# A two-block transformer step on one core: softmax order in the attention, half buffers and late splits for the weights, and the skip term of the S5 mixer folded into its taps

## The chip, the cores and the metric

The kernel runs on one core of a Trainium2 chip. The metric is the device time of one launch in microseconds (us), median over the runs shown. The profile is of one execution of the program with the hardware profiler on.

## The reference, cut to what matters

Two blocks follow each other on a sequence of 256 positions with 1024 channels, all in float32. Each has two layers.

```
first:  h = h + short_conv_mixer(rmsnorm(h));  h = h + mlp(rmsnorm(h));  h = h + ple(rmsnorm(h), p[0])
        h = h + dilated_attention(rmsnorm(h)); h = h + mlp(rmsnorm(h));  h = h + ple(rmsnorm(h), p[1])
second: h = h + 0.5 swiglu(rmsnorm(h)); h = h + s5_mixer(rmsnorm(h));  h = h + 0.5 swiglu(rmsnorm(h))
        shared keys and values = rmsnorm(h) @ w_kv, some compressed
        h = h + 0.5 swiglu(rmsnorm(h)); h = h + nsa_attention(rmsnorm(h), kv);  h = h + 0.5 swiglu(rmsnorm(h))

dilated_attention, per head: three groups with dilations 1, 4, 16 share one softmax
  s = q k^T / sqrt(128), masked to a band;  p = exp(s - lse);  o = sum over groups of weight * (p v)
S5 mixer: x_t = A x_(t-1) + B u_t  (64 groups of 16 channels, 64 states)
  y = Re(C x) + d_skip * u;   y = gelu(y);   y * sigmoid(y @ w_glu)
swiglu: (silu(x @ w_a) * (x @ w_b)) @ w_out
rmsnorm(x) = x * rsqrt(mean(x^2) + eps) * gain
```

## The kernel before, in words

**Products.** Activations lie transposed, channels on the partitions, 256 positions on the free axis. A float32 product is made of three matmuls in a reduced format: each operand is split into a high part (`hi`) and a low rest (`lo`), and `mm3` (L328 on) issues hi·hi, lo·hi and hi·lo into one PSUM sum. They are lines L333, L334 and L335 of the profile.

**Weights.** All weight matrices stand in HBM as one row of pieces of 128 x 2048 elements (1 MB). `load` fetches them (tile `raw`), `split` makes `whi` on ScalarE (L267) and `wlo` on VectorE (L271), two halves of 1024 columns each; the four pieces after the S5 mixer's own are subtracted on GpSimd instead (L269, set `BY_POOL`). Each of `raw`, `whi`, `wlo` has a ring of three buffers. `piece` hands out the next split piece to a matmul block and, before it does so, splits up to three pieces ahead.

**Norms.** The factor of a norm isn't waited for: the matmuls run on the unscaled input, and a PSUM result is multiplied by the factor R afterwards. `norm_step` counts pairs of k tiles inside the matmul loops; at the first count the sums of squares are taken (`norm_ssq`), at the fifth a matmul spreads the factor over the partitions (L509, tile `misc`), ScalarE copies it out (L511, tile `R`). Evacuations that need R are put on the list `late` until then (`when_scaled`).

**Order.** A scheduler of the framework sorts the recorded instructions by a simulated timeline. Where the code says `in_order()`, an instruction is held behind the one recorded last on its engine. Each engine then works in that order and waits on semaphores.

**Attention** (L700 to L850). For each of eight heads: q, k, v pieces for three groups; rotary on q and k (VectorE L733 and L735, GpSimd L736, L738, L739, then `qh`, `ql`); v (`vh`, `vl`, L413, L414). `head` is a generator: scores, then the masked softmax (VectorE L771 to L779, ScalarE L781 exp, GpSimd L782 reciprocal, ScalarE L784 scaling), then the transposes of the probabilities on TensorE (L789 to L791), then the products with v. The `yield`s between them let the loop over pieces put matmuls of the next head in between.

**S5 mixer** (L1140 to L1330). The input h (tile `XG`, L1148, scaled by the gain) is transposed on TensorE (L1171), multiplied by the norm factor and goes through four quarter chains: `w` (input taps), `c` (rotation by GpSimd L1222 and L1226, VectorE L1220, L1221, L1227, scan L1223, result `sX` L1230), `t` and `o` (taps and output). `skip` multiplies XG by R on GpSimd (L1254, eight times), after ScalarE has multiplied it by d (L1279). `result` transposes the output back, adds XG (L1268), applies Gelu (L1272) and splits it (tiles `yh`, `yl`). The order of these steps is the string `S5_SEQ`. Then the GLU's matmuls follow, then the next SwiGLU, whose first input `xh`, `xl` is line L460.

Of the kernel before, what the change touches and what calls it, by code (L numbers as in the profile page):

```python
# [10 lines left out]
F32 = mybir.dt.float32  # L11
# [6 lines left out]
D = 1024  # L18
S = 256
# [29 lines left out]
SC_HEAD = SC_D + KT  # L49
# [6 lines left out]
S5_SEQ = "r0 r1 w0 r2 w1 r3 c0 w2 t0 c1 o0 w3 t1 t2 T o1 c2 t3 K o2 c3 R0 o3 R1 S"  # L56
# [143 lines left out]

BY_POOL = {S5_AT + S5_N + i for i in range(4)}
# [9 lines left out]
IN_ORDER = {E.DVE, E.Activation, E.Pool, E.PE}  # L211


class Ker:
    def __init__(self, ctx, tc, a):
# [13 lines left out]
        self.by_pool = BY_POOL  # L229
# [3 lines left out]
    def load(self, i):  # L233
        nc = self.nc
        while self.n_load < min(i, len(PLAN)):
            n, e = self.n_load, PLAN[self.n_load]
            if e[0] == "s5":

                m = (n - S5_AT) % 3
                t = self.ring.tile([128, NP_], F32R if m else F32, name=("raw", "whi", "wlo")[m])  # L240
                t = t.bitcast(F32) if m else t
                nc.sync.dma_start(t, self.s5w[e[1:]])
# [14 lines left out]
    def split(self, i):  # L257
        nc = self.nc
        while self.n_split < min(i, len(PLAN)):
            n = self.n_split  # L260
            assert PLAN[n][0] != "s5"
            self.load(n + 1)
            r = self.raw.pop(n)
            hi = self.ring.tile([128, NP_], F32R, name="whi")
            lo = self.ring.tile([128, NP_], F32R, name="wlo")
            for c in (slice(i, i + 1024) for i in range(0, NP_, 1024)):
                nc.scalar.activation(hi[:, c], r[:, c], AF.Copy)  # L267
                if n in self.by_pool:
                    nc.gpsimd.tensor_tensor(lo[:, c], r[:, c], hi[:, c].bitcast(F32), op=OP.subtract)  # L269
                else:  # L270
                    nc.vector.tensor_sub(lo[:, c], r[:, c], hi[:, c].bitcast(F32))  # L271
            self.spl[n] = (hi, lo)
            self.n_split += 1

    def piece(self, *want, ahead=3):
# [20 lines left out]
    def step(self):  # L296
# [3 lines left out]
        while self.credit >= 1.0:  # L300
# [36 lines left out]
    def cols_open(self, *want, ahead=3, ps="acc"):  # L337
        wh, wl = (w.rearrange("p (k c) -> p k c", k=KT) for w in self.piece("cols", *want, ahead=ahead))
        return self.psum(ps).rearrange("p (o t) -> p o t", o=2), wh, wl

    def cols_part(self, x, a, ks):
        acc, wh, wl = a
        for k in ks:
            for o in range(2):
                s = slice(128 * o, 128 * o + 128)
                self.mm3(acc[:, o], wh[:, k, s], wl[:, k, s], x[0][k], x[1][k],
# [9 lines left out]
    def cols_t(self, x, *want, ps="acc"):  # L356
        wh, wl = (w.rearrange("p (k c) -> p k c", k=KT) for w in self.piece("cols", *want))
        acc = self.psum(ps).rearrange("p (o t) -> p o t", o=2)
        for k in range(KT):
            for o in range(2):  # L360
                s = slice(128 * o, 128 * o + 128)
                self.mm3(acc[:, o], x[0][k][:, s], x[1][k][:, s], wh[:, k], wl[:, k],
# [30 lines left out]
    def rows(self, hid, dn, first, last, outs, *want):  # L393
        wh, wl = (w.rearrange("p (k c) -> p k c", k=2) for w in self.piece("rows", *want))
        for o in outs:
            for k in range(2):
                s = slice(128 * o, 128 * o + 128)
                self.mm3(dn[o // 2][:, o % 2], wh[:, k, s], wl[:, k, s], hid[0][:, k], hid[1][:, k],
                         first and k == 0 and o % 2 == 0, last and k == 1)
# [146 lines left out]
    def first_feed(self):  # L546
# [3 lines left out]
        hi, lo = (self.ring.tile([128, NP_], F32R, name=f"w{c}") for c in ("hi", "lo"))  # L550
        for j in range(4):
# [3 lines left out]
            self.hilo(r[:, c], hi[:, c], lo[:, c])  # L555
# [94 lines left out]
    def ple_proj(self, l, p):  # L650
# [3 lines left out]
        wh, wl = (w.rearrange("p (k c) -> p k c", k=2) for w in self.piece("rows", "ple_w_proj", l, 0))  # L654
        for j in range(4):
            acc = self.psum().rearrange("p (o t) -> p o t", o=2) if j > 1 else accs[j]
            for o in range(2):
                for k in range(2):
                    s = slice(256 * j + 128 * o, 256 * j + 128 * o + 128)
                    self.mm3(acc[:, o], wh[:, k, s], wl[:, k, s], p[0][:, k], p[1][:, k],  # L660
# [52 lines left out]
    def attention_(self, x):  # L713
# [40 lines left out]
        def head(h):  # L754
# [279 lines left out]
    def s5_weights(self, qs):  # L1034
# [5 lines left out]
        for q in qs:  # L1040
# [18 lines left out]
            for hf in range(2):  # L1059
# [46 lines left out]
                taps(1)  # L1106
                yield
# [29 lines left out]
    def s5(self, upd):  # L1137
# [3 lines left out]
        XG = big("XG", [2, 8, 4, 32])  # L1141
# [58 lines left out]
        wp = lambda n, q: self.piece("s5", n, q).rearrange("p (g c) -> p g c", c=128)  # L1200
# [37 lines left out]
        def wo(q):  # L1238
# [5 lines left out]
            for i in range(2):  # L1244
                evac(0, YP[0][:, :, 4 * q + 2 * i:4 * q + 2 * i + 2].rearrange("p j g h -> p g j h"),
# [617 lines left out]
```

## Time and profile before

| | |
|---|---|
| median of 3 runs | 1875.27 us (1873.52 to 1877.62) |
| profiled execution, its own time | 1871.9 us |
| its span | 1870.1 us |
| TensorE busy | 1817.1 us, 97% |
| VectorE / ScalarE / GpSimd busy | 69% / 50% / 25% |
| mean granted TensorE clock | 0.989 of 2.4 GHz |

TensorE works almost all the time. Time is lost in short waits of TensorE (a few us each) and in the short stretches at half the clock that come behind some of them. In 40 slices of the span, the busy share of TensorE is 9 tenths or more but for the first slice and two slices around 1050 to 1100 us, where the S5 mixer lies.

### The profile page before, as it was taken

The numbers are of one execution on the slowest core, as the hardware profiler recorded it, in microseconds if no ns is written. First come the engines' busy times: TensorE is split into PE (matmuls) and PEld (weight loads), VectorE is DVE, ScalarE is ACT, GpSimd is POOL, SyncE is SP. The second block draws the span as 40 slices with busy tenths as digits, with TensorE's granted clock in tenths as the row PEclk, the third lists the DMA queues.
The fourth block names the chain that finished last, engine by engine and source line by source line (L and its number), as shares of the span: only waits on it lengthen the run. The fifth ranks groups of instructions, "written<-read, shape, count | busy, mean of one in ns | idle before, by whom it ended". The sixth has DMA issues, their size and how long they took to land.

```text
span 1870.1 us, 35822 instructions
## 1 busy us (share of the span) xinstructions
PE 1817.1 (97%) x15244; PEld 1792.0 (96%) x15244; DVE 1281.1 (69%) x1633; ACT 942.3 (50%) x1442; POOL 468.5 (25%) x392
## 2 busy tenths in 40 slices
PE   8999999999999999999999779999999999999999
PEld 8999999999999999999999779999999999899999
DVE  6889887888776867778555566555785556875554
ACT  4365556555444555466443455444565445764442
POOL 2120012564652311112010442101243113421110
PEclk9999999999999999999999979999999999999999
DMA  6455666443343576666555734755455453445452
GB/s 253 181 187 209 220 223 219 161 152 142 136 144 127 198 236 227 219 207 254 188 186 187 291 128 172 263 185 186 174 187 200 173 183 118 65 161 181 181 180 90
DMA packets 78927, 344.68 MB, mean 184 GB/s; under 512 B 8022, under 2 KB 34378, under 8 KB 41392
## 3 DMA queue, kind: packets, MB, share of 16 engines
q1 hardware_dynamic: 77616, 339.30, 52.4%
q0 software_dynamic: 1008, 2.91, 0.4%
q8 instruction: 119, 1.95, 0.4%
q14 instruction: 40, 0.33, 0.1%
q10 hardware_dynamic: 144, 0.20, 0.0%
HBM read 328.71 MB, written 17.86 MB: 185 GB/s over the span
## 4 chain that ended last, share of the span: by engine, by line
PE 81%; DVE 7%; POOL 4%; issue 3%; ACT 2%; DMA 1%; SPq 0%; POOLq 0%; ACTq 0%; DVEq 0%
PE acc L334 16%; PE acc L335 16%; PE acc L333 16%; PE big L333 9%; PE big L334 9%; PE big L335 9%; DVE wlo L271 3%; POOL qks L736 2%; POOL qkt L739 1%; PE acc L1690 1%; POOL qkc L738 1%; ACT whi L267 1%; DMA bias<-zb 1%; PE big L1673 1%; PE misc L485 0%
## 5 line engine op out<-in xcount | busy, mean ns | idle before, releaser
L267 ACT ACTIVATE whi<-raw 128x1024 fp32r<-128x1024 f32 x558 | 559.8, 1051 | 599.8 <-issue 360.9
L271 DVE TENSOR_TENSOR wlo<-raw,whi 128x1024 fp32r<-128x1024 f32 x550 | 698.7, 1305 | 224.5 <-ACT whi L267 223.9
L334 PE MATMUL acc<-xl,whi 128*128 128x256 f32 x2096 | 595.7, 285 | 3.6 <-DVE xl L460 3.0
L333 PE MATMUL acc<-xh,whi 128*128 128x256 f32 x2096 | 594.5, 285 | 4.5 <-ACT whi L410 2.3
L335 PE MATMUL acc<-xh,wlo 128*128 128x256 f32 x2096 | 595.8, 285 | 3.0 <-DVE wlo L411 2.8
L333 PEld LDWEIGHTS acc<-xh,whi 128*128 128x128 f32 x2096 | 403.2, 193 | 6.4 <-ACT whi L410 2.7
L335 PEld LDWEIGHTS acc<-xh,wlo 128*128 128x128 f32 x2096 | 403.8, 193 | 5.3 <-DVE wlo L411 3.4
L334 PEld LDWEIGHTS acc<-xl,whi 128*128 128x128 f32 x2096 | 403.8, 193 | 4.8 <-DVE xl L460 3.4
L334 PE MATMUL big<-hl,whi 128*128 128x256 f32 x1216 | 343.6, 283 | 0.0
L335 PE MATMUL big<-hh,wlo 128*128 128x256 f32 x1216 | 343.2, 283 | 0.0
L333 PE MATMUL big<-hh,whi 128*128 128x256 f32 x1216 | 341.1, 284 | 0.0
L334 PEld LDWEIGHTS big<-hl,whi 128*128 128x128 f32 x1216 | 232.8, 191 | 0.5 <-issue 0.5
L335 PEld LDWEIGHTS big<-hh,wlo 128*128 128x128 f32 x1216 | 232.7, 191 | 0.2 <-issue 0.2
L333 PEld LDWEIGHTS big<-hh,whi 128*128 128x128 f32 x1216 | 231.0, 191 | 1.9 <-issue 1.9
L855 POOL TENSOR_TENSOR e<-e,R 128x512 f32<-128x512 f32 x44 | 80.6, 1833 | 524.5 <-ACT e L854 524.5
L335 PE MATMUL acc<-yh,wlo 128*128 128x256 f32 x720 | 204.1, 285 | 1.2 <-DVE wlo L271 1.0
L334 PE MATMUL acc<-yl,whi 128*128 128x256 f32 x720 | 204.1, 286 | 1.0 <-DVE yl L460 0.6
L333 PE MATMUL acc<-yh,whi 128*128 128x256 f32 x720 | 203.0, 286 | 0.8 <-ACT yh L410 0.5
L334 PEld LDWEIGHTS acc<-yl,whi 128*128 128x128 f32 x720 | 138.7, 193 | 2.0 <-DVE yl L460 1.3
L335 PEld LDWEIGHTS acc<-yh,wlo 128*128 128x128 f32 x720 | 138.9, 193 | 1.7 <-DVE wlo L271 1.2
L333 PEld LDWEIGHTS acc<-yh,whi 128*128 128x128 f32 x720 | 138.1, 194 | 2.2 <-ACT yh L410 1.3
L516 DVE TENSOR_TENSOR e<-acc,R 128x512 f32<-128x512 f32 x54 | 36.9, 689 | 84.4 <-PE acc L335 84.1
(440 smaller groups left out, 2592.4 us busy)
## 6 DMA issues: line engine op xcount, KB each, us to landing
raw<-in_wst SPq DMA_DIRECT2D x277, 1024.0 KB, 4.9
s5wo<-b SPq DMA_DIRECT2D x8, 512.0 KB, 5.7
s5wi<-wi SPq DMA_DIRECT2D x16, 256.0 KB, 3.7
s5to<-s5k SPq DMA_DIRECT2D x32, 128.0 KB, 4.5
bias<-zb SPq DMA_DIRECT2D x16, 256.0 KB, 4.5
cbt<-zb SPq DMA_DIRECT2D x4, 900.0 KB, 6.5
raw<-s5to SPq DMA_DIRECT2D x3, 1024.0 KB, 4.8
raw<-in_wst SPq DMA_DIRECT2D x4, 512.0 KB, 7.9
```

The source lines that it names most:

```text
L267: nc.scalar.activation(hi[:, c], r[:, c], AF.Copy)
L271: nc.vector.tensor_sub(lo[:, c], r[:, c], hi[:, c].bitcast(F32))
L333: mm(out, lh, rh, start=first, stop=False, skip_group_check=True)
L334: mm(out, lh, rl, start=False, stop=False, skip_group_check=True)
L335: mm(out, ll, rh, start=False, stop=last, skip_group_check=True)
L516: self.nc.vector.tensor_tensor(t, acc, self.bc2(self.R), op=OP.mult)
L736: nc.gpsimd.tensor_tensor(s, s, bc(self.rS), op=OP.mult)
L738: nc.gpsimd.tensor_tensor(c, t[:32], bc(self.rC), op=OP.mult)
L739: nc.gpsimd.tensor_tensor(t[:32], c, s, op=OP.add)
L855: nc.gpsimd.tensor_tensor(T[i], T[i], self.bc2(self.R), op=OP.mult)
L1673: nc.tensor.transpose(tp[:, 128 * n:128 * n + 128], blocks[4 * i + n], self.ident)
L1690: nc.tensor.matmul(o[:, dst], w, t[lp][:, e, b, src], start=False, stop=(b == 1 and kb == 1 and i == 2), skip_group_check=True)
```

## The change

Five things change.

1. In `head` the scores and the products with v are placed `in_order()`, the pause between scores and softmax is gone (another stands behind the softmax), and the nine transposes of a head are one ordered block with three PSUM tiles.
2. `whi` and `wlo` of a piece become two tiles of half the columns each (class `Halves`, ring of six).
3. Splits have places. `piece` puts the fetch of the next pieces (load and split) behind the evacuations on `late` while a norm factor is being made, in order; background steps pause as well. GpSimd makes no `wlo` any more.
4. `rows` walks over k first for all but the last block, so that the first half buffer is used up first.
5. In S5 the term d·u is added to the taps (`dd`, small products on GpSimd in the background work of an earlier stage), and `skip`, XG·d and the addition of XG go. Gelu moves into the evacuation of the output (L1163 before). XG lies in an outer pool. The three first GLU pieces are split at two named places (P and Q in `S5_SEQ`).

The core of the diff:

```diff
-S5_SEQ = "r0 r1 w0 r2 w1 r3 c0 w2 t0 c1 o0 w3 t1 t2 T o1 c2 t3 K o2 c3 R0 o3 R1 S"
+S5_SEQ = "r0 r1 w0 r2 w1 r3 T c0 w2 t0 c1 o0 w3 t1 t2 o1 c2 t3 o2 c3 P R0 o3 R1 Q S"
-BY_POOL = {S5_AT + S5_N + i for i in range(4)}
+class Halves:
+    def __init__(self, pool, name):
+        self.t = [pool.tile([128, NP_ // 2], F32R, name=name, bufs=6) for _ in range(2)]
...
-        self.split(min(i + ahead, self.cap))
-        self.load(i + ahead + 3 if d >= 0 or i + ahead < S5_AT else min(S5_AT + 3 * (i + ahead - S5_AT) + 3, S5_AT + 9))
+        def fetch():
+            self.split(min(i + ahead, self.cap))
+            self.load(i + ahead + 3 if d >= 0 or i + ahead < S5_AT
+                      else min(S5_AT + 3 * (i + ahead - S5_AT) + 3, S5_AT + 9))
+
+        if 0 < len(self.todo) < 4 and self.n_split >= i + 2:
+
+            self.late.append(lambda: self.behind(fetch))
+        else:
+            fetch()
...
-        while self.credit >= 1.0:
+        while self.credit >= 1.0 and not self.todo:
...
+    def behind(self, fn):
+        with self.in_order():
+            fn()
...
-        for o in outs:
-            for k in range(2):
-                s = slice(128 * o, 128 * o + 128)
+        for k, o in ([(k, o) for o in outs for k in range(2)] if last else [(k, o) for k in range(2) for o in outs]):
+            s = slice(128 * o, 128 * o + 128)
...
-                    self.mm3(dst[g], qh[:, 0, q0:q0 + 128], ql[:, 0, q0:q0 + 128],
-                             qh[:, 1, :nk], ql[:, 1, :nk], first, True)
-            yield
+                    with self.in_order():
+                        self.mm3(dst[g], qh[:, 0, q0:q0 + 128], ql[:, 0, q0:q0 + 128],
+                                 qh[:, 1, :nk], ql[:, 1, :nk], first, True)
...
             yield
+            yield
             PT = []
-            for g in range(3):
-                tp = self.psum("big")
-                nc.tensor.transpose(tp[:, 0:128], p0[:, g], self.ident)
...
+            with self.in_order():
+                tps = [self.psum("big") for _ in range(3)]
+                for g, tp in enumerate(tps):
+                    nc.tensor.transpose(tp[:, 0:128], p0[:, g], self.ident)
...
+                dd = bp.tile([16, 8, 16], F32, name="dd", bufs=1)
+                gp.tensor_tensor(dd, self.ident[:16, None, :16].to_broadcast([16, 8, 16]),
+                                 self.small[:16, SC_D + g0:SC_D + g0 + 8, None].to_broadcast([16, 8, 16]), op=OP.mult)
+                gp.tensor_tensor(ksb[:, :, :16], ksb[:, :, :16], dd, op=OP.add)
...
-        def skip():
-            self.norm_bc()
-            Ri = self.R.rearrange("p (c i) -> p i c", i=8)
-            for k in range(KT):
-                t = XG[:, k // 4, :, k % 4]
-                gp.tensor_tensor(t, t, Ri, op=OP.mult)
+        def presplit(c):
+            with self.in_order():
+                if c == 0:
+                    split.extend(self.split_open(3))
+                self.split_half(split, c)
...
-                v.tensor_tensor(dst[:, 4 * jb:4 * jb + 4], tp.rearrange("p (j g c) -> p j g c", j=4, c=32),
-                                XG[:, hf, 4 * jb:4 * jb + 4], op=OP.add)
-            for g in range(0, 4, 2):
-                k = 4 * hf + g
-                ac.activation(Y[0][:, k:k + 2], Y[0][:, k:k + 2], AF.Gelu_apprx_tanh)
+                evac(1 - jb, dst[:, 4 * jb:4 * jb + 4], tp.rearrange("p (j g c) -> p j g c", j=4, c=32))
```

ScalarE at the norm of the SwiGLU behind S5, before: R stands between splits, and the following piece was split ahead of it (`misc` is the spread factor, `e2` the Silu, `R` the factor, `whi` and `raw` weight pieces).

```order
L847 ACTIVATE e2_13026<-acc_12968 128x512
L267 ACTIVATE whi_13101<-raw_12859 128x1024 x2
L267 ACTIVATE whi_13163<-raw_12966 128x1024 x2
L511 ACTIVATE R_13053<-misc_13051 128x256
L854 ACTIVATE e2_13057<-e0_13055 128x512
L854 ACTIVATE e2_13160<-e0_13158 128x512
L267 ACTIVATE whi_13225<-raw_13034 128x1024 x2
L410 ACTIVATE hh_13097<-e2_13057 128x512
```

The same place in the changed kernel.

```order
L433 ACT_TABLE_LOAD
L433 ACTIVATE tab_13314<-ones_76 128x1
L879 ACTIVATE e2_13384<-acc_13326 128x512
L539 ACTIVATE R_13403<-misc_13401 128x256
L886 ACTIVATE e2_13407<-e0_13405 128x512
L289 ACTIVATE whi_13410<-raw_13213 128x1024
L289 ACTIVATE whi_13411<-raw_13213 128x1024
L289 ACTIVATE whi_13461<-raw_13215 128x1024
L289 ACTIVATE whi_13462<-raw_13215 128x1024
L289 ACTIVATE whi_13525<-raw_13324 128x1024
L289 ACTIVATE whi_13526<-raw_13324 128x1024
L886 ACTIVATE e2_13522<-e0_13520 128x512
```

Six `whi` halves now stand behind R and the Silu that needs it; whi_13410 is the half piece that TensorE uses next.

TensorE there, in the changed kernel: `misc_13401` is the matmul that spreads the factor, `acc` the two gate sums.

```order
L362 MATMUL acc_13471<-xh7_13017,whi_13317 128x256
L537 MATMUL misc_13401<-dg_13399,ones_76 128x256
L363 MATMUL acc_13471<-xl7_13025,whi_13317 128x256
L364 MATMUL acc_13471<-xh7_13017,wlo_13319 128x256
L362 MATMUL acc_13471<-xh7_13017,whi_13317 128x256
L363 MATMUL acc_13471<-xl7_13025,whi_13317 128x256
L364 MATMUL acc_13471<-xh7_13017,wlo_13319 128x256
L362 MATMUL acc_13535<-xh0_13010,whi_13410 128x256
L363 MATMUL acc_13535<-xl0_13018,whi_13410 128x256
L364 MATMUL acc_13535<-xh0_13010,wlo_13412 128x256
```

Six matmuls stand between the spread and the first that needs whi_13410; before, the pieces for 100 more matmuls were split ahead of R.

ScalarE in the softmax of the fourth head pair's first head, before (`p1`, `p0` the scores of one head, `sm` their sums, `nm` their negative maxima).

```order
L781 ACTIVATE p1_6735,sm_6742<-p1_6735,nm_6741 128x768
L781 ACTIVATE p0_6736,sm_6742<-p0_6736,nm_6741 128x384
L267 ACTIVATE whi_6750<-raw_6519 128x1024 x2
L784 ACTIVATE p1_6735<-p1_6735,sm_6742 128x768
L784 ACTIVATE p0_6736<-p0_6736,sm_6742 128x384
L267 ACTIVATE whi_6843<-raw_6588 128x1024
```

The same place in the changed kernel.

```order
L809 ACTIVATE p1_6846,sm_6853<-p1_6846,nm_6852 128x768
L809 ACTIVATE p0_6847,sm_6853<-p0_6847,nm_6852 128x384
L289 ACTIVATE whi_6933<-raw_6697 128x1024
L812 ACTIVATE p1_6846<-p1_6846,sm_6853 128x768
L812 ACTIVATE p0_6847<-p0_6847,sm_6853 128x384
L289 ACTIVATE whi_7027<-raw_6768 128x1024
```

One half piece instead of two stands between the exponentials and the scalings.

GpSimd through the S5 mixer, before.

```order
L475 TENSOR_TENSOR rcol<-rmean,mhalf 128x2
L506 TENSOR_TENSOR dg<-cst,rcol 128x256
L1254 TENSOR_TENSOR XG<-XG,R 128x8x32 x8
L1222 TENSOR_TENSOR sZ<-sZ,sZs 128x512 x2
L1226 TENSOR_TENSOR sw<-sw,tC 128x512 x2
L1222 TENSOR_TENSOR sZ<-sZ,sZs 128x512
L269 TENSOR_TENSOR wlo<-raw,whi 128x1024 x2
L1229 MEMSET sX 128x16
L1222 TENSOR_TENSOR sZ<-sZ,sZs 128x512
L1229 MEMSET sX 128x16
L269 TENSOR_TENSOR wlo<-raw,whi 128x1024 x6
```

And in the changed kernel.

```order
L1267 MEMSET sX 128x16 x2
L503 TENSOR_TENSOR rcol<-rmean,mhalf 128x2
L1260 TENSOR_TENSOR sZ<-sZ,sZs 128x512 x2
L1264 TENSOR_TENSOR sw<-sw,tC 128x512 x2
L1260 TENSOR_TENSOR sZ<-sZ,sZs 128x512
L1267 MEMSET sX 128x16
L1260 TENSOR_TENSOR sZ<-sZ,sZs 128x512
L1267 MEMSET sX 128x16
L482 TENSOR_TENSOR sq<-sq,sqt 128x512 x2
```

XG and all `wlo` are gone from GpSimd; the rest keeps its order.

## Rows read from the trace of the kernel before

**Rows 1.** the page, busy time of each engine and instruction counts.

```profile
PE 1817.1 (97%) x15244; PEld 1792.0 (96%) x15244; DVE 1281.1 (69%) x1633; ACT 942.3 (50%) x1442; POOL 468.5 (25%) x392
```

**Rows 2.** the page, costliest groups: busy, mean ns, idle before and its releaser.

```profile
L267 ACT ACTIVATE whi<-raw 128x1024 fp32r<-128x1024 f32 x558 | 559.8, 1051 | 599.8 <-issue 360.9
L271 DVE TENSOR_TENSOR wlo<-raw,whi 128x1024 fp32r<-128x1024 f32 x550 | 698.7, 1305 | 224.5 <-ACT whi L267 223.9
```

**Rows 3.** waits of TensorE, attention from 350 to 590 us: total, times, longest.

```profile
PE big L789 <- ACT p L784: 9.6, 4, 2.5
PE big L334 <- DVE ql L411: 1.2, 1, 1.2
```

**Rows 4.** windows: length, then PE, PEld, DVE, ACT, POOL busy (count), clock, DMA share, GB/s.

```profile
460.00:590.00 130.00, 124.03 (x1027) 123.48 (x1026) 99.45 (x134) 64.19 (x100) 73.47 (x40) 0.99 0.40 140
1060.00:1080.00 20.00, 10.12 (x216) 7.86 (x208) 16.21 (x13) 9.49 (x16) 16.95 (x13) 0.82 0.73 285
1080.00:1100.00 20.00, 16.12 (x139) 14.43 (x140) 12.30 (x15) 9.44 (x19) 8.71 (x4) 0.66 0.24 92
```

**Rows 5.** windows, TensorE alone (busy, count, clock), behind two of those waits.

```profile
507.00:513.00 6.00, 5.22 (x44) 1.00 0.32 106
573.00:579.00 6.00, 5.18 (x31) 0.72 0.32 105
```

**Rows 6.** timeline of ScalarE at a softmax: start, length, operation, idle before.

```profile
572.34 1.42 ACT L784 ACTIVATE p<-p,sm 128x768 f32<-128x768 f32 x2
```

**Rows 7.** timeline of VectorE before that softmax.

```profile
562.81 0.69 DVE L411 TENSOR_TENSOR ql<-qkt,qh 128x512 fp32r<-128x512 f32 x1 [4.44 <-ACT qh L410]
...
563.81 0.68 DVE L771 SCALAR_TENSOR_TENSOR p<-big,masks 128x512 f32<-128x512 f32 x1
```

**Rows 8.** timeline of GpSimd, rotary of the same head.

```profile
555.50 4.01 POOL L738 TENSOR_TENSOR qkc<-qkt,rC 32x512 f32<-32x512 f32 x1 [2.13 <-DVE qkt L733]
559.48 1.28 POOL L736 TENSOR_TENSOR qks<-qks,rS 32x512 f32<-32x512 f32 x1
```

**Rows 9.** timeline of GpSimd in S5.

```profile
1055.63 6.64 POOL L1254 TENSOR_TENSOR XG<-XG,R 128x256 f32<-128x256 f32 x8 [5.23 <-ACT R L511]
1062.22 2.52 POOL L1222 TENSOR_TENSOR sZ<-sZ,sZs 128x512 f32<-128x512 f32 x2
...
1072.51 5.11 POOL L269 TENSOR_TENSOR wlo<-raw,whi 128x1024 fp32r<-128x1024 f32 x2
```

**Rows 10.** timeline of VectorE in S5.

```profile
1058.74 0.68 DVE L1221 TENSOR_TENSOR sZs<-acc,tS 128x512 f32<-128x512 f32 x1
...
1072.54 2.85 DVE L1230 TENSOR_TENSOR sX<-sw,sws 128x512 f32<-128x512 f32 x1
...
1091.20 0.69 DVE L1230 TENSOR_TENSOR sX<-sw,sws 128x512 f32<-128x512 f32 x1
```

**Rows 11.** timeline of ScalarE at the start of S5.

```profile
1044.07 5.31 ACT L1148 ACTIVATE XG<-h,small 128x256 f32<-128x256 f32 x8 [9.20 <-DVE sq L1156]
```

**Rows 12.** timeline of TensorE where the GLU ends and the SwiGLU begins.

```profile
1116.39 0.28 PE L335 MATMUL acc<-yh,wlo 128*128 128x256 f32 x1
...
1119.92 0.39 PE L334 MATMUL acc<-xl,whi 128*128 128x256 f32 x1 [3.02 <-DVE xl L460]
```

**Rows 13.** timeline of TensorE, spread of that SwiGLU's norm factor.

```profile
1139.55 0.59 PE L509 MATMUL misc<-dg,ones 128*128 128x256 f32 x2
```

**Rows 14.** timeline of ScalarE behind it.

```profile
1141.42 0.36 ACT L511 ACTIVATE R<-misc 128x256 f32<-128x256 f32 x1
1143.60 1.29 ACT L854 ACTIVATE e<-e 128x512 f32<-128x512 f32 x2 [1.81 <-DVE e L516]
```

**Rows 15.** timeline of VectorE, first rotary of the attention.

```profile
349.87 1.28 DVE L733 TENSOR_TENSOR qkt<-acc,R 128x512 f32<-128x512 f32 x2
```

**Rows 16.** timeline of ScalarE, the split that follows it.

```profile
354.63 0.63 ACT L410 ACTIVATE qh<-qkt 128x512 fp32r<-128x512 f32 x1
```

**Rows 17.** timeline of TensorE, second matmul block behind the attention.

```profile
639.42 0.58 PE L333 MATMUL acc<-xh,whi 128*128 128x256 f32 x1 [2.11 <-DVE e L625]
```

More of the change, by code (lines that the diff above doesn't have):

```diff
@@ L239, in load @@
                 m = (n - S5_AT) % 3
-                t = self.ring.tile([128, NP_], F32R if m else F32, name=("raw", "whi", "wlo")[m])
-                t = t.bitcast(F32) if m else t
-                nc.sync.dma_start(t, self.s5w[e[1:]])
+                if m:
+                    t = [a.bitcast(F32) for a in Halves(self.ring, ("whi", "wlo")[m - 1]).t]
+                else:
+                    t = self.ring.tile([128, NP_], F32, name="raw")
+                    t = [t[:, :NP_ // 2], t[:, NP_ // 2:]]
+                for i in range(2):
+                    nc.sync.dma_start(t[i], self.s5w[e[1:]][:, NP_ // 2 * i:NP_ // 2 * (i + 1)])
             else:
@@ L257, in split, with split_open, split_half @@
     def split(self, i):
-        nc = self.nc
         while self.n_split < min(i, len(PLAN)):
-            n = self.n_split
+            todo = self.split_open(1)
+            for c in range(2):
+                self.split_half(todo, c)
+    def split_open(self, m):
+        todo = []
+        for n in range(self.n_split, self.n_split + m):
             assert PLAN[n][0] != "s5"
             self.load(n + 1)
[L263 to L273, printed above, removed]
+            self.spl[n] = tuple(Halves(self.ring, w) for w in ("whi", "wlo"))
+            todo.append((self.raw.pop(n), *self.spl[n]))
+        self.n_split += m
+        return todo
+    def split_half(self, todo, c):
+        nc = self.nc
+        for r, hi, lo in todo:
+            rc = r[:, NP_ // 2 * c:NP_ // 2 * (c + 1)]
+            nc.scalar.activation(hi.t[c], rc, AF.Copy)
+            nc.vector.tensor_sub(lo.t[c], rc, hi.t[c].bitcast(F32))
     def piece(self, *want, ahead=3):
@@ L337, in cols_open @@
     def cols_open(self, *want, ahead=3, ps="acc"):
-        wh, wl = (w.rearrange("p (k c) -> p k c", k=KT) for w in self.piece("cols", *want, ahead=ahead))
+        wh, wl = self.piece("cols", *want, ahead=ahead)
         return self.psum(ps).rearrange("p (o t) -> p o t", o=2), wh, wl
@@ L393, in rows @@
     def rows(self, hid, dn, first, last, outs, *want):
[L394 to L399 removed]
+        wh, wl = self.piece("rows", *want)
+        for k, o in ([(k, o) for o in outs for k in range(2)] if last else [(k, o) for k in range(2) for o in outs]):
+            s = slice(128 * o, 128 * o + 128)
+            self.mm3(dn[o // 2][:, o % 2], wh.at(k, 2)[:, s], wl.at(k, 2)[:, s], hid[0][:, k], hid[1][:, k],
+                     first and k == 0 and o % 2 == 0, last and k == 1)
     def table(self, fn):
@@ L549, in first_feed @@
         r = self.raw.pop(0)
-        hi, lo = (self.ring.tile([128, NP_], F32R, name=f"w{c}") for c in ("hi", "lo"))
+        hi, lo = (Halves(self.ring, n) for n in ("whi", "wlo"))
         for j in range(4):
@@ L653, in ple_proj @@
         pp = [self.pair(f"pp{j}", 1) for j in range(4)]
-        wh, wl = (w.rearrange("p (k c) -> p k c", k=2) for w in self.piece("rows", "ple_w_proj", l, 0))
+        wh, wl = self.piece("rows", "ple_w_proj", l, 0)
         for j in range(4):
@@ L1661, in transposes @@
         def transposes(j):
-            th, tl = (self.ring.tile([128, NP_], F32R, name=f"w{c}") for c in ("hi", "lo"))
+            th, tl = (Halves(self.ring, n).t for n in ("whi", "wlo"))
             blocks = []
```

68 lines of the change are left out of this document (38 added, 30 removed).

## The prediction

> **What bounds the kernel now.** I read the page's head first: TensorE is busy 1817.1 us of a span of 1870.1 us, 97% [rows 1]. A matmul costs 0.121 us wherever it runs undisturbed (124.03 us for 1027 of them [rows 4]), and the change leaves their number as it is but for one. So the 53 us in which TensorE is idle, and the stretches at half clock, are all there is to win, and each new wait of TensorE is a loss at full price. Next I read TensorE's waits with its timeline, to see where these 53 us lie. Three places matter. In the attention, four waits for the scaled probabilities, 9.6 us together [rows 3]. In the S5 mixer, TensorE is busy 10.12 of 20 us, then 16.12 of 20 at a clock of 0.66 [rows 4]. Behind the GLU it stands from 1116.5 to 1119.92 us [rows 12], and behind the attention 2.11 us at 639.42 us [rows 17]. Last the windows behind a wait: the 6 us behind one attention wait ran at a granted clock of 0.72 and held 31 matmuls, those behind another ran at 1.00 and held 44 [rows 5]. The difference, 13 x 0.121 = 1.6 us, is what a dip to the lower level costs here; of the four attention waits, whose windows read like one or the other of these, two have one.
>
> **S5 mixer: gain 11.5 us.** Three pieces of its chain go. First, XG on ScalarE began at 1044.07 after an idle time of 9.20 us, and its eight instructions take 5.31 us, with the transposes behind them [rows 11]. In an outer pool they need not wait for the stage's end; each follows its own part of h. Two of eight stay behind the last part, so at most 6/8 x 5.31 = 4.0 us go and at least none; the norm's factor is late next, so I take 2.5. Second, GpSimd's eight XG products hold it until 1062.22, where its first sZ sum starts, while VectorE had the operand done at 1058.74 + 0.68 = 1059.42 [rows 9, 10]: 2.8 us. Third, the GpSimd wlo at 1072.51 (5.11 us) stands ahead of the last sZ sum, and beside it sX on VectorE takes 2.85 us, against 0.69 for the same instruction at 1091.20 [rows 9, 10]. The two delays are 5.1 + 2.2 = 7.3 us; the chain is interleaved with others, so between 3 and 7.3, I take 6.2. The last sX then ends at 91.9 - 11.5 = 1080.4 us. The GLU's end follows it: 1116.5 - 1091.9 = 24.6 us later before, and its 192 matmuls alone are 23.2 us, so that distance can't shrink; it can grow, since P puts three halves (3 x 1.05 on ScalarE, 3 x 1.3 on VectorE [rows 2]) ahead of the first result, where splits of the same kind lay before. Hence the range of this term: 6 to 14. The d·u term moved into the taps adds 16 small GpSimd instructions in an early stage where GpSimd is idle most of the time (25% busy over the span [rows 1]): nothing, at most 1 us if a tap is late.
>
> At the third piece a rule of the Trainium skill bears. VectorE and GpSimd delay each other here: the rotary's first product takes 4.01 us on GpSimd beside two wlo, the second, alike in size, 1.28 us [rows 8]. The skill's page "SBUF — State Buffer" (section "Who interferes with whom") says that a VectorE instruction with two SBUF inputs and a GpSimd instruction that reads SBUF lock each other out for the whole instruction, the first to issue winning. By that rule GpSimd's Silu products would meet the late wlo more often, since these now come right behind R. If each of the first products at three norms waited for one wlo of 1.3 us, the sum would be 3.9 us worse; no row shows that meeting, and I leave it out.
>
> **Start of the SwiGLU behind the GLU: gain 4.0 us.** The wait is for xl on VectorE (3.0 us [rows 12]), which stands behind four wlo halves in the order; the changed one has two between h and xl. The wait and its dip are 3.0 + 1.6; I leave 0.6.
>
> **Behind the attention: gain 3.7 us.** The 2.11 us are for an evacuation on VectorE that waits behind splits [rows 17]. Splits now stand behind the evacuation: 2.1 + 1.6. Nothing else is late there, as R is early.
>
> **Attention: gain 5.2 us.** Before the scaling, ScalarE makes two whi halves; in the changed order one, 1.05 us less [rows 2, 6]. VectorE makes one wlo less between p and the maxima, 1.3 us [rows 2]. But the transposes now stand 96 matmuls behind the scores instead of 105, 1.1 us sooner. So 1.05 + 1.3 - 1.1 = 1.25 us at best; the exponentials and the sums of GpSimd lie between, so I take 0.9 for each of four waits, 3.6, and one of the two dips, 1.6. The early start of the softmax gives nothing by itself: p begins at 563.81 because ql ahead of it waited 4.44 us for the rotary [rows 7, 8], and ql stands ahead of p in the new order too. Bounds: 0, and 9.6 + 3.2 = 12.8 if the waits go.
>
> **The late splits: loss 19.8 us.** Where a norm's factor is being made, the next piece is now split behind R, and TensorE comes to it soon. From the spread matmul (0.59 us [rows 13]) R starts 0.65 us later at best and takes 0.36 [rows 14]; so 1.0. An evacuation e is 0.69 (p, a VectorE instruction of the same shape [rows 7]), a Silu 1.29 / 2 = 0.65 [rows 14], whi 1.05, wlo 1.3 [rows 2]; the third product, which needs wlo, comes 0.24 us behind the first. Before, Silu started 1.81 us behind R's end [rows 14], 1.1 more than e alone, so that each chain may be 1.1 us longer. Per place, with the matmuls that the new order has between the spread and the first use:
> - SwiGLU behind the GLU, 6 matmuls (0.7 us): 1.0 + 0.7 + 0.65 + 1.05 + 1.3 = 4.7, less 0.24 and 0.7, 3.7 us.
> - The first SwiGLU of that block, 21 matmuls (2.5): 2.0 us.
> - The projection to the shared keys and values, 3 matmuls (0.4), no Silu: 1.0 + 1.05 + 1.3 - 0.24 - 0.4 = 2.7, and a second piece two matmuls on, 0.7: 3.4 us.
> - The attention's first pieces, 32 matmuls (3.9): qh stands ahead of whi on ScalarE, and came 4.76 us behind qkt's start [rows 15, 16]; 1.0 + 4.8 + 0.6 + 1.05 + 1.3 = 8.7, less 0.24 and 3.9: 4.6 us.
> - The second MLP, 41 matmuls (5.0): 1.0 + 2 x 0.69 + 2 x 0.65 + 1.05 + 1.3 = 6.1: 0.9 us.
> - The two gated projections, 31 and 38 matmuls (3.8 and 4.6): 1.0 + 1.05 + 1.3 = 3.4, no wait for the split; VectorE, which makes the next input after these wlo, is later: 0 to 3 us, I take 1.0 each.
> - Dips: three of these waits are as long as the attention's; two of three, 3.2 us.
>
> That is 3.7 + 2.0 + 3.4 + 4.6 + 0.9 + 2.0 + 3.2 = 19.8; from 8 (chains hidden by PSUM slots that I don't see) to 26 (1.1 us at six places more).
>
> Half buffers and the order in `rows` let a matmul start on half a piece; in steady stages TensorE waits for no split [rows 4], so nothing. The NSA attention has a few more small instructions (a chunk is split at the half): 0 to 1 us, taken as nothing.
>
> **Sum.** -11.5 - 4.0 - 3.7 - 5.2 + 19.8 = -4.6 us. The profiled execution took 1871.9 us, 3.4 under the median of the three runs; I put the difference on the median: 1875.3 - 4.6 = 1870.7 us.
>
> **Rivals.**
> - The late splits decide. Condition: R reaches ScalarE no sooner than before, so that each of the six places costs 1.1 more (26 us), and S5 gives 6 because P and Q hold up the first result, attention 2, the others 7.7. Net 26 - 15.7 = +10: 1885. For it: six matmuls between spread and use are certain in the order; against: R's wait for splits ahead of it is gone. It decides from losses above 24.4 us on.
> - The path wins in full. S5 14, attention 12.8, the two waits 8.3, late splits 17: -18: 1857. For it: the S5 stretch has 9.9 + 3.9 us idle in 40 us and a clock of 0.66 [rows 4]. Against: the rotary still holds p.
> - No change: the attention keeps its waits, since p and ql stand as before, and the rest is as forecast: +0.6: 1876. For it: [rows 7]; against: one split less ahead of the scaling.
>
> **Chances.** Forecast 0.40 (1864 to 1874), full gain 0.20, no change 0.20, slower 0.20. The range 1857 to 1884 leaves out about 2 in 10, half on each side. What a measurement can tell from no change is 0.2%, 3.75 us. Faster by more: 0.30 + 0.20 = 0.50; within: 0.08 of the forecast and 0.16 of the no-change case, 0.24; slower: the rest, 0.26.
>
> **What would show it.** In S5, the last sX near 1080 us minus the shift before it, GpSimd without XG and wlo, and the GLU's end some 25 us later. At each of the places of the late splits a wait of TensorE on whi or wlo of 2 to 5 us that before hadn't; without them the loss was mis-sized. In the attention the waits for p at 1.5 us each, ql still ahead of p. Wrong is the prediction if the S5 stretch isn't at least 6 us shorter, or the late splits cost under 10 us.

## The result and the profile after

| | before | changed |
|---|---|---|
| median | 1875.63 us (4 runs, 1873.52 to 1877.62) | 1886.61 us (4 runs, 1883.12 to 1888.64) |
| ratio | | 1.0062, 95% interval 1.005 to 1.0074 |
| profiled execution, span | 1870.1 us | 1884.7 us |

The change made the kernel slower by 11 us; 1870.7 us was forecast, with a range up to 1884. TensorE stayed at 97% of the span [rows 1]:

```profile
PE 1824.6 (97%) x15242; PEld 1798.8 (95%) x15242; DVE 1293.1 (69%) x1647; ACT 956.5 (51%) x1438; POOL 466.5 (25%) x391
```

Both kernels issue the same matmuls within each stage, but for two in S5 (the spread of the norm's factor for XG) that the change takes away; they are left out. So I sorted TensorE's instructions of each trace by start and took, at the ends of stages, the n-th start of one less the n-th start of the other. The growth of that difference over a stage is what the stage lost (+) or won (-), waits and clock together. All such numbers below are made this way, from one profiled execution of each kernel; the unit is us. "Late fetch" is the load and split of the next pieces put behind a norm's factor (point 3 of the change).

| stage (us in the trace before) | changed | no late fetch | late fetch behind others only | no GpSimd wlo | skip term and no GpSimd wlo |
|---|---|---|---|---|---|
| start and first mixer, to 263 | +0.8 | -0.6 | +1.3 | -0.2 | +1.2 |
| first MLP, to 315 | +2.0 | +0.8 | +2.0 | 0.0 | 0.0 |
| first gated projection, to 335 | +4.5 | -1.6 | -1.6 | 0.0 | 0.0 |
| attention's start, to 361 | +7.3 | +0.1 | +9.5 | 0.0 | 0.0 |
| attention, to 621 | -4.6 | -2.6 | -4.5 | 0.0 | -0.1 |
| behind the attention, to 649 | -3.7 | -2.6 | -3.8 | -0.2 | 0.0 |
| second MLP, to 842 | +1.0 | +0.7 | +1.4 | -0.1 | +1.8 |
| second gated projection, to 854 | +7.4 | -0.2 | -0.2 | 0.0 | 0.0 |
| first SwiGLU, to 1042 | +0.9 | +4.2 | +5.6 | 0.0 | 0.0 |
| S5 and GLU, to 1116 | -9.5 | -7.9 | -8.0 | -2.4 | -4.5 |
| start of the next SwiGLU, to 1130 | -4.8 | -4.8 | -4.8 | -4.7 | -4.7 |
| rest of that SwiGLU, to 1322 | +5.0 | 0.0 | +5.3 | 0.0 | 0.0 |
| keys and values, to 1573 | +4.9 | +1.1 | +4.0 | -0.1 | 0.0 |
| NSA, to 1639 | +3.0 | +2.5 | +0.4 | -0.4 | +0.2 |
| all, to TensorE's last start | +14.3 | -11.0 | +6.6 | -8.3 | -6.2 |

The texts that stood ahead of the experiments had one boundary at 1122 us, inside the start of that SwiGLU, and so name 12.9 won up to there and 4.0 lost behind it.

The other columns are experiments below. In the changed kernel the places that were to win won 22.6 us, 24.4 were forecast. The places of the late splits lost 30.0 (4.5 + 7.3 + 7.4 + 0.9 + 5.0 + 4.9), 19.8 were forecast. The waits of TensorE show them (engine, line, releaser; us in total, times, longest):

```profile
PE big L819 <- ACT p L812: 8.2, 4, 2.8
PE big L362 <- ACT whi L289: 5.7, 3, 3.1
...
PE acc L362 <- ACT xh L441: 3.5, 1, 3.5
PE acc L362 <- ACT whi L289: 2.7, 2, 2.3
...
PE acc L362 <- DVE e L544: 2.4, 1, 2.4
...
PE big L364 <- DVE wlo L290: 2.0, 1, 2.0
PE acc L364 <- DVE wlo L290: 2.0, 2, 1.0
...
PE acc L363 <- DVE xl L442: 1.5, 1, 1.5
```

The first answers to [rows 3], 9.6 us before: little has gone. Before, there was none on whi of L267 and one of 1.0 us on wlo of L271; xh, xl and e belong to the gated projections. Where they stand, by TensorE's timeline (start, length, operation, idle before it):

```profile
357.31 0.39 PE L362 MATMUL big<-xh,whi 128*128 128x256 f32 x1 [3.09 <-ACT whi L289]
...
359.82 0.58 PE L364 MATMUL big<-xh,wlo 128*128 128x256 f32 x1 [2.00 <-DVE wlo L290]
...
861.63 1.01 PE L362 MATMUL acc<-xh,whi 128*128 128x256 f32 x3 [3.52 <-ACT xh L441]
...
864.13 0.58 PE L363 MATMUL acc<-xl,whi 128*128 128x256 f32 x1 [1.50 <-DVE xl L442]
...
1143.66 0.39 PE L362 MATMUL acc<-xh,whi 128*128 128x256 f32 x1 [2.29 <-ACT whi L289]
...
1145.15 0.58 PE L364 MATMUL acc<-xh,wlo 128*128 128x256 f32 x1 [0.98 <-DVE wlo L290]
...
1340.12 0.39 PE L362 MATMUL big<-yh,whi 128*128 128x256 f32 x1 [1.18 <-ACT whi L289]
...
1342.01 0.39 PE L362 MATMUL big<-whi,yh 128*128 128x256 f32 x1 [1.39 <-ACT whi L289]
```

At 1143.66 and 1145.15 the matmuls behind the spread are used up (five in the trace, the forecast counted six) and whi, then wlo, are awaited: 3.3 us, 3.7 was worked out. At 861.63 TensorE waits for an input that nothing in the forecast priced above 3 us. ScalarE in the second gated projection of the changed kernel tells why:

```profile
848.80 0.38 ACT L539 ACTIVATE R<-misc 128x256 f32<-128x256 f32 x1 [9.36 <-PE misc L537]
849.08 4.84 ACT L289 ACTIVATE whi<-raw 128x1024 fp32r<-128x1024 f32 x5
853.82 1.14 ACT L704 ACTIVATE e<-e 128x512 f32<-128x512 f32 x2
...
861.09 0.49 ACT L441 ACTIVATE xh<-h,gg 128x256 fp32r<-128x256 f32 x1
```

And the same stretch before:

```profile
842.30 0.37 ACT L511 ACTIVATE R<-misc 128x256 f32<-128x256 f32 x1
844.48 0.63 ACT L676 ACTIVATE e<-e 128x512 f32<-128x512 f32 x1 [1.81 <-DVE e L516]
```

Five whi stand between R and the first sigmoid; it comes 5.0 us behind R instead of 2.2. VectorE has five wlo ahead of its third product with R:

```profile
849.22 1.29 DVE L544 TENSOR_TENSOR e<-acc,R 128x512 f32<-128x512 f32 x2 [4.87 <-ACT R L539]
850.42 6.86 DVE L290 TENSOR_TENSOR wlo<-raw,whi 128x1024 fp32r<-128x1024 f32 x5
857.20 0.68 DVE L544 TENSOR_TENSOR e<-acc,R 128x512 f32<-128x512 f32 x1
```

The gated projection's evacuations are not on the list `late`: they are issued when the next stage asks for its input. So the fetch, appended to an empty list, runs first and takes ScalarE for 4.8 us and VectorE for 6.9.

In S5, GpSimd has no XG and no wlo, where before it had both [rows 9], and the last sX stands at 1094.01 us, 34.7 us behind the first transposes of S5. Before it was 44.3 (1091.20 [rows 10] less 1046.89), and those transposes had waited 3.0 us. TensorE at the start of S5, before:

```profile
1043.62 0.28 PE L335 MATMUL big<-hh,wlo 128*128 128x256 f32 x1
1046.89 1.06 PE L1171 MATMUL big<-cst,XG 128*128 128x128 f32 x8 [2.99 <-DVE sq L1156]
```

And in the changed kernel:

```profile
1059.22 0.28 PE L364 MATMUL big<-hh,wlo 128*128 128x256 f32 x1
1059.34 0.93 PE L1208 MATMUL big<-cst,XG 128*128 128x128 f32 x7
```

From the matmul ahead of S5 to the last sX it is 34.8 us instead of 47.6. GpSimd's sums in the changed kernel:

```profile
1072.33 1.27 POOL L1260 TENSOR_TENSOR sZ<-sZ,sZs 128x512 f32<-128x512 f32 x1 [6.47 <-DVE sZs L1259]
...
1086.90 1.26 POOL L1260 TENSOR_TENSOR sZ<-sZ,sZs 128x512 f32<-128x512 f32 x1 [2.34 <-DVE sZs L1259]
```

GpSimd now waits for VectorE, not the other way. The last sX on VectorE:

```profile
1094.01 0.69 DVE L1268 TENSOR_TENSOR sX<-sw,sws 128x512 f32<-128x512 f32 x1
```

### The profile page after: what moved, and what is told of

The parts are those of the page before. It is cut to its first block, busy times and chain, and to the rows that moved or that the text cites. A ratio compares the mean times of both kernels' runs of the same rounds, so it can differ in the third digit from the quotient of the medians.

```text
span 1884.7 us, 36094 instructions
## 1 busy us (share of the span) xinstructions
PE 1824.6 (97%) x15242; PEld 1798.8 (95%) x15242; DVE 1293.1 (69%) x1647; ACT 956.5 (51%) x1438; POOL 466.5 (25%) x391
## 4 chain that ended last, share of the span: by engine, by line
PE 76%; DVE 8%; POOL 7%; ACT 4%; issue 3%; DMA 2%; SPq 0%; POOLq 0%; ACTq 0%; DVEq 0%
PE acc L364 15%; PE acc L363 15%; PE acc L362 15%; PE big L364 9%; PE big L363 8%; PE big L362 8%; POOL qkt L767 3%; POOL qks L764 3%; DVE wlo L290 2%; POOL qkc L766 2%; ACT whi L289 1%; PE acc L1724 1%; ACT qh L438 1%; DMA s5wi<-wi 1%; PE misc L513 1%
## 5 line engine op out<-in xcount | busy, mean ns | idle before, releaser
L290 DVE TENSOR_TENSOR wlo<-raw,whi 128x1024 fp32r<-128x1024 f32 x558 | 709.7, 1283 | 312.4 <-ACT whi L289 308.9
L289 ACT ACTIVATE whi<-raw 128x1024 fp32r<-128x1024 f32 x558 | 581.2, 1056 | 538.7 <-PE acc L363 277.2
L887 POOL TENSOR_TENSOR e<-e,R 128x512 f32<-128x512 f32 x44 | 74.0, 1681 | 555.1 <-ACT e L886 545.9
L482 POOL TENSOR_TENSOR sq<-sq,sqt 128x512 f32<-128x512 f32 x27 | 41.6, 1540 | 138.8 <-ACT sqt L481 138.2
```

The costliest lines, as they stand in the source:

```text
L289: nc.scalar.activation(hi.t[c], rc, AF.Copy)
L290: nc.vector.tensor_sub(lo.t[c], rc, hi.t[c].bitcast(F32))
L482: nc.gpsimd.tensor_tensor(self.sq, self.sq, s, op=OP.add)
L887: nc.gpsimd.tensor_tensor(T[i], T[i], self.bc2(self.R), op=OP.mult)
```

## The experiments

All were timed beside the kernel before on the same chip.

| kernel | median us (runs) | ratio to before, 95% |
|---|---|---|
| changed | 1886.61 (4) | 1.0062, 1.005 to 1.0074 |
| changed, no late fetch | 1860.14 (4) | 0.9918, 0.9898 to 0.9939 |
| changed, no pause of the background | 1888.61 (4) | 1.007, 1.0051 to 1.009 |
| changed, old head | 1885.91 (4) | 1.0052, 1.0032 to 1.0073 |
| before, skip term in the taps | 1872.86 (10) | 0.9995, 0.9981 to 1.0009 |
| changed, late fetch behind others only | 1879.22 (10) | 1.0024, 1.0014 to 1.0034 |
| before, no wlo on GpSimd | 1867.14 (5) | 0.9958, 0.9943 to 0.9972 |
| before, skip term in the taps, no wlo on GpSimd | 1865.88 (4) | 0.9957, 0.9941 to 0.9973 |
| changed, late fetch in the first SwiGLU only | 1862.49 (4) | 0.9941, 0.9921 to 0.996 |
| changed, no late fetch, no pause | 1859.14 (4) | 0.9918, 0.9898 to 0.9938 |
| changed, no late fetch, old rows | 1860.14 (4) | 0.9919, 0.9903 to 0.9934 |

**No late fetch.**

```diff
-        if 0 < len(self.todo) < 4 and self.n_split >= i + 2:
+        if False:
```

> The changed kernel, but the fetch of the next piece is never put behind a norm factor; all else stays. Theory A, the late splits: by the n-th matmul of both traces they cost 4.5 + 7.0 us around the first gated projection and the attention's start, 8.9 around the second, 4.0 and 4.7 at the SwiGLU behind S5 and at the shared keys and values, 29 in all, and gave 3.6 back behind the attention. Without them 1886.6 - 25 = 1861 us, and TensorE's waits on whi and wlo (L289, L290) and for xh there are gone. Rival B, half buffers and the ordered, paused background crowd the same places whoever is late: a third returns, 1878 us, and the waits move rather than go.

1860.14 us: theory A, to 1 us. The waits on whi and wlo (L289, L290) are gone, as are those for xh and xl of the gated projections. The three longest of TensorE's waits left between 300 and 900 us:

```profile
PE big L819 <- ACT p L812: 8.2, 3, 3.7
PE acc L362 <- ACT e L886: 3.1, 1, 3.1
PE big L363 <- DVE ql L439: 1.4, 1, 1.4
```

In the second gated projection the first sigmoid is 1.8 us behind R again:

```profile
835.68 0.38 ACT L539 ACTIVATE R<-misc 128x256 f32<-128x256 f32 x1
836.27 1.06 ACT L289 ACTIVATE whi<-raw 128x1024 fp32r<-128x1024 f32 x1 [0.21 <-PE acc L363]
837.48 1.23 ACT L704 ACTIVATE e<-e 128x512 f32<-128x512 f32 x2
```

Two things did not go as written. The gain behind the attention was to be given back, and 2.6 of 3.7 us stay (table), so the late fetch had not made most of it. And the first SwiGLU loses 4.2 us without the late fetch, where the changed kernel lost 0.9. TensorE now comes to it without the delay of the gated projection ahead of it, and waits for its Silu (the 3.1 us on e above).

**No pause of the background.**

```diff
-        while self.credit >= 1.0 and not self.todo:
+        while self.credit >= 1.0:
```

> The changed kernel, but the background steps don't pause while a norm factor is being made. Theory: the pause pushes the S5 tables' work to the end of the first MLP, where TensorE waits twice for VectorE's b (1.2 us each at 275 and 291 us): 2 us back, 1884.6. Rival: these waits come from the moved splits, the pause is worth nothing: 1886.6, both waits still there.

1888.61 us, not to be told from the changed kernel. In the profiled execution the first MLP is 2.5 us shorter and both waits for b are gone, so the pause makes them; but the first gated projection is 3.6 us longer, with waits of 2.8 for xh and 2.9 for xl. What makes these was not followed; with neither pause nor late fetch the place loses nothing (-0.6, experiment below). Theory right on the place, wrong on the sum.

**Old head.**

```diff
-                    with self.in_order():
-                        self.mm3(dst[g], qh[:, 0, q0:q0 + 128], ql[:, 0, q0:q0 + 128],
-                                 qh[:, 1, :nk], ql[:, 1, :nk], first, True)
+                    self.mm3(dst[g], qh[:, 0, q0:q0 + 128], ql[:, 0, q0:q0 + 128],
+                             qh[:, 1, :nk], ql[:, 1, :nk], first, True)
+            yield
...
-            yield
             yield
             PT = []
-            with self.in_order():
-                tps = [self.psum("big") for _ in range(3)]
...
```

> The changed kernel with the attention's head() of before (scores, softmax, transposes and products in the order and with the pauses of before). Theory: the 4.3 us that the attention won come from the head, mostly one split less ahead of the scaling: 1886.6 + 4.3 = 1891. Rival: they come from the half pieces alone: 1886.6, four waits for p of 2.0 us on average as in the changed kernel.

1885.91 us, and the stage of the attention keeps 4.4 us of the 4.6 that it won. TensorE's wait for p is 7.4 us in all, shorter than with the new head:

```profile
PE big L817 <- ACT p L812: 7.4, 3, 2.9
```

The rival is right that the rewritten head is worth nothing here. That the half pieces alone win the 4.6 us is not shown: without the late fetch 2.6 of them are left (table).

**Skip term alone, on the kernel before.**

```diff
-S5_SEQ = "r0 r1 w0 r2 w1 r3 c0 w2 t0 c1 o0 w3 t1 t2 T o1 c2 t3 K o2 c3 R0 o3 R1 S"
+S5_SEQ = "r0 r1 w0 r2 w1 r3 T c0 w2 t0 c1 o0 w3 t1 t2 o1 c2 t3 o2 c3 R0 o3 R1 S"
...
+                gp.tensor_tensor(ksb[:, :, :16], ksb[:, :, :16], dd, op=OP.add)
...
-        XG = big("XG", [2, 8, 4, 32])
+        XG = self.XG
...
```

> The kernel before with only the S5 part that has to do with the skip term: d in the taps, no XG products, XG in the outer pool, Gelu in the evacuation; whole buffers, no P and Q, four pieces of wlo still on GpSimd. Theory: the XG part is about half of the 12.9 us that S5 and the SwiGLU's start won, since GpSimd's wlo still delay the chain and sX: 1875.6 - 6 = 1869.6. Rival: the skip term was all of it, 1862.7, and GpSimd's wlo stand where nobody waits.

No change that can be measured (1872.86 us). S5 wins 1.1 us and the start of the next SwiGLU 3.4, but 3.2 go in the second MLP, where the new order makes TensorE wait 2.3 us for an input, and 1.4 in the attention. In S5 TensorE now stands still for 10.69 us:

```profile
1080.75 1.94 PE L1200 MATMUL big<-whi,sX 128*32 128x128 f32 x32 [10.69 <-issue]
...
1087.94 0.32 PE L1200 MATMUL big<-wlo,sX 128*32 128x128 f32 x4 [3.54 <-POOL wlo L269]
```

GpSimd's timeline there:

```profile
1069.04 2.36 POOL L269 TENSOR_TENSOR wlo<-raw,whi 128x1024 fp32r<-128x1024 f32 x1 [2.27 <-ACT whi L267]
1071.36 1.71 POOL L1227 TENSOR_TENSOR sZ<-sZ,sZs 128x512 f32<-128x512 f32 x1
...
1073.08 2.34 POOL L269 TENSOR_TENSOR wlo<-raw,whi 128x1024 fp32r<-128x1024 f32 x1
1075.38 2.17 POOL L1231 TENSOR_TENSOR sw<-sw,tC 128x512 f32<-128x512 f32 x1
```

Two wlo stand ahead of chain products. But they are only a part of the cause. With these wlo on VectorE (experiment "Both" below) TensorE still waits 7.83 us there for sX:

```profile
1076.92 1.94 PE L1200 MATMUL big<-wlo,sX 128*32 128x128 f32 x32 [7.83 <-DVE sX L1235]
```

So GpSimd's wlo cost about 3 us at this place, and the rest of the wait is there without them.

**No wlo on GpSimd, on the kernel before.**

```diff
-BY_POOL = {S5_AT + S5_N + i for i in range(4)}
+BY_POOL = set()
```

> The kernel before with the four pieces of wlo of GpSimd made on VectorE; nothing else. Theory: GpSimd's wlo delay the last sZ sum and sX by up to 7.3 us, so S5 is 4 to 6 us shorter: 1870. Rival: the four pieces cost VectorE as much there (8 x 1.3 us in the same stretch), or the XG products hold the chain anyway: no change, 1874.

1867.14 us: 8 us for one line, more than the theory gave it, and not only where it looked. S5 wins 2.4 us (6.2 was the forecast's term for it); 4.7 come at the start of the next SwiGLU, where the wait of 3.0 us for xl [rows 12] is gone. The second chain's sX takes 0.68 us again, 2.85 before [rows 10]:

```profile
1073.56 0.68 DVE L1230 TENSOR_TENSOR sX<-sw,sws 128x512 f32<-128x512 f32 x1
```

The last sX comes 4.9 us sooner, counted from where TensorE falls idle ahead of S5. Half of that is lost again where the GLU begins, for there TensorE waits for its input (0.54 us before):

```profile
1085.60 0.80 PE L333 MATMUL acc<-yh,whi 128*128 128x256 f32 x2 [6.64 <-ACT yh L410]
```

**Both, on the kernel before.** The two diffs above together.

> The kernel before with the skip term in the taps and GpSimd's four wlo pieces on VectorE, without half buffers, placed splits or the new head. Theory: with GpSimd free in S5 the stretch wins what the changed kernel wins there, 11 to 13 us by the n-th matmul, where the skip term alone won 4.5 and left TensorE waiting 11 us behind GpSimd: 1874 - 10 = 1864, and the half buffers and P and Q are worth little. Rival: S5 needs the placed halves P and Q: no more than 6 us there, 1869.

1865.88 us, between theory and rival; S5 and the start of the next SwiGLU win 4.5 + 4.7 us, of which 1.8 go in the second MLP. The skip term adds 2.1 us in S5 to the one line, and nothing measurable to the time. The changed kernel without late fetch wins 7.9 in S5; 3.4 of these are therefore due to the half buffers, P and Q or the order that comes of them; which, was not tried.

**Late fetch behind others only.**

```diff
-        if 0 < len(self.todo) < 4 and self.n_split >= i + 2:
+        if 0 < len(self.todo) < 4 and self.n_split >= i + 2 and self.late:
```

> The changed kernel, but the fetch is put off only where an evacuation already stands on the late list; in the gated projections, whose evacuations are not on it, the split is made at once. Theory: there the late fetch lands between R and the evacuations that need it, five whi halves ahead of the first sigmoid; so these two places, 4.5 and 7.4 us, come back, and the attention's start, the SwiGLUs and the keys and values keep their waits: 1886.6 - 12 = 1874.6. Rival: whatever is split late costs the same, and only the first piece of each norm moves: 1882.

1879.22 us, between theory and rival. The two gated projections give back 6.1 and 7.6 us: the late fetch is the cause there, shown. That it does so by standing ahead of the evacuations is read from the order in the timelines above; no run has the fetch late and behind them. But the attention's start is 2.2 us longer and the first SwiGLU 4.7, so half was only passed on; the wait for whi is now 5.3 us at its longest:

```profile
PE big L362 <- ACT whi L289: 7.9, 3, 5.3
...
PE acc L362 <- ACT whi L289: 5.0, 2, 2.8
```

**Late fetch in the first SwiGLU only.**

```diff
+        if 0 < len(self.todo) < 4 and self.n_split >= i + 2 and PLAN[i][1:3] == ("ffn1_w_in_2", 0):
```

> The changed kernel with the late fetch at one place only, the first SwiGLU. Without any late fetch TensorE waits there 3.5 us at 872.78 for the Silu, whose factor R stands behind a split; with it the changed kernel lost 1.1 us there. Theory: this place alone wins 2 to 3 us over the kernel without late fetch, 1860.1 - 2.5 = 1857.6. Rival: the wait for whi that replaces it is as long: 1860.

1862.49 us: the rival. The stage is 5.0 us longer than before instead of 4.2. Even where a split stands ahead of R, splitting behind it did not help.

**No late fetch, no pause.** Both diffs of the first two experiments.

> The changed kernel without late fetch and without the pause of the background steps. Theory: behind the attention the 2.1 us wait for e went because background work no longer stands ahead of e on VectorE while the factor is being made; late fetch or pause alone does that, and with neither the wait is back, 2.6 us, while the first MLP wins 0.8: 1860.1 + 2 = 1862. Rival: half buffers did it, the wait stays gone: 1859.

1859.14 us: the rival. With neither, the gain behind the attention stays (-3.5 us). It belongs to the half buffers or the order that comes with them.

**No late fetch, old rows.**

```diff
-        for k, o in ([(k, o) for o in outs for k in range(2)] if last else [(k, o) for k in range(2) for o in outs]):
+        for k, o in [(k, o) for o in outs for k in range(2)]:
```

> The changed kernel without late fetch, and with rows() walking as before (both k of one output block, then the next), so that both halves of a piece are needed at once. Theory: in these stages a split is done long before its use (no wait for whi or wlo in the steady stages of either trace), so the order in rows is worth nothing: 1860, the same waits. Rival: it is what keeps the second halves hidden behind the attention and in the MLPs: 1863 to 1866, with new waits for wlo at the pieces' starts.

1860.14 us, the same as with the new walk, stage by stage within 0.8 but for the clock in the NSA attention: worth nothing, as expected.

The version without late fetch beats both kernels, with or without the pause: 1860.1 and 1859.1 us.

## Why the prediction was wrong

**The step that failed is the term "the late splits: loss 19.8 us", and in it the two gated projections at "1.0 each".** The term's places lost 30.0 us in the profiled execution, dips included; without the late fetch the same places lose 3.6, and taking it away gave 26.5 us by the medians. By part:

- Where the sum followed a chain behind the spread matmul, it came near. The SwiGLU behind S5 was to lose 3.7 without its dip; the waits are 2.29 + 0.98 and the stage lost 5.0. Keys and values: 3.4 forecast, waits of 1.18 + 1.39, 4.9 lost. The attention's start: 4.6 forecast, waits of 3.09 + 2.00, 7.3 lost.
- The first SwiGLU (2.0 forecast, 0.9 lost) is no proof of its chain. TensorE came to it 7.4 us late from the gated projection; where that delay is gone, the stage loses 4.2 without a late fetch and 5.0 to 5.6 with one.
- "The two gated projections ... no wait for the split; VectorE, which makes the next input after these wlo, is later: 0 to 3 us, I take 1.0 each" failed. They lost 4.5 and 7.4. I asked which pieces TensorE would miss, and not what the five splits behind R would hold up on ScalarE and VectorE. The first sigmoid is 2.8 us later, and five wlo (6.86 us) stand ahead of VectorE's third product with R; at 1.0 each I priced less than one of them. In the profiled executions this one step is 9.9 of the 18.9 us between forecast and result. Undone alone (late fetch behind others only) it gives 7.4 us by the medians, because a part of the delay then appears at the next places.
- The second MLP was to lose 0.9 and shows no such wait.

**Attention, 5.2 us forecast, 4.6 measured, for another reason.** The head, from which I worked it out, is worth nothing; p waits 8.2 us, 0.35 less per wait, not 0.9. Without late fetch, and with the new head, the attention wins 2.6. That ql holds p [rows 7] was right.

**Behind the attention, 3.7 us forecast and 3.7 measured, also for another reason.** I gave it to the late fetch; without late fetch and pause it is still 3.5.

**S5 and the SwiGLU's start, 11.5 + 4.0 forecast, 9.5 + 4.8 measured.** The place was right and the sums nearly; the parts were not, so that the agreement is in part luck. The last sX came 12.8 us sooner (34.8 against 47.6 us behind the matmul ahead of S5). But the GLU's last matmul, which the forecast let follow it at the old distance (its range allowed for more), starts 28.5 us behind it instead of 25.2. GpSimd's wlo alone are worth 2.4 in S5, against 6.2; the skip term and XG alone 1.1, against 2.5 + 2.8; both together 4.5. Another 3.4 came with the half buffers, P and Q or their order, which I had priced at nothing, and the last 1.6 only beside the late fetch (9.5 against 7.9). The start of the SwiGLU wins 4.7 to 4.8 in every kernel without wlo on GpSimd and 3.4 with the skip term alone, so it doesn't need the half buffers. In each of these fewer wlo stand between the h before it and xl on VectorE (two or three instead of four), as the forecast had it; no experiment was made on that wait alone. That GpSimd's wlo and sX delay each other was right: the single sX went from 2.85 to 0.68 us when the wlo left GpSimd. The Trainium skill's rule on the shared port ("SBUF — State Buffer", section "Who interferes with whom") agrees with this delay.

**What was priced at nothing.** The first MLP lost 2.0 us, to the pause of the background steps beside the late fetch (without the pause it wins 0.5; without the late fetch the pause costs 0.8). The NSA attention lost 3.0 us to a stretch at half clock; that code is the same in kernels with and without it, and it isn't counted to the change (below).

**The rival "the late splits decide"** put the time at 1885 and was nearest. Its place and its threshold (losses above 24.4 us) were right, and its reason, R coming no sooner, was not: R starts 0.41 us after its second spread matmul does at ten of eleven norms, 0.41 to 2.29 before, and the splits behind it did the harm. The late fetch wasn't needed for that: without it R starts as soon at nine of eleven. The rival had 0.20.

Of the two signs of being wrong that the prediction named, neither came: S5 is more than 6 us shorter, and the late splits cost more than 10. It had no sign for a cost far above its sum.

## What to carry to other kernels

When work is moved behind a signal, list everything on the same engines that also waits for that signal, and price the move at its queue place there, not only at its consumer: here five splits went ahead of a sigmoid that had waited as long as they. Try taking long optional work off an engine that a serial chain uses in between (GpSimd's wlo in S5, 8 us for one line) before rewriting the chain, and look where the gain falls: here more than half of it was not in the chain but at a wait behind it. And undo the parts one at a time: the same change held a loss of 26 us and a gain of 15.

## What the runs showed of the hardware

A dip of TensorE's clock can come or not behind a wait of the same length at the same matmul. In the NSA attention TensorE waits 1.6 to 1.9 us at one matmul in all of these kernels. In the changed kernel the 12 us behind it ran at a granted clock of 0.57 (TensorE's busy time and count, clock):

```profile
1601.00:1613.00 12.00, 11.45 (x46) 0.57 0.29 49
```

Before, the stretch behind that wait ran at full clock:

```profile
1590.00:1602.00 12.00, 10.07 (x65) 1.00 0.42 69
```

Of the kernels with half buffers, three show this dip (the changed one, without late fetch, old head), the other five don't. The stage lost 2.5 to 3.7 us with it and 0.1 to 0.6 without, and the difference is more than half of the 0.2% that a measurement can tell. What decides it stays open.
